# A two-layer convolution, attention and expert trunk: weight splits and sigmoids moved among the gate tiles

## The chip, the cores and the metric

The kernel runs on one core of one Trainium2 chip. The metric is the device time of the kernel in microseconds (us), from several timed executions; one more execution was recorded by the hardware profiler. The core has a matrix engine (TensorE, PE in the profile, its weight loads PEld), three engines for elementwise work (VectorE or DVE, ScalarE or ACT, GpSimd or POOL), SyncE (SP), whose queue issues most transfers here, and DMA engines that move data between HBM and the on-chip memory (SBUF). Matrix products land in PSUM banks. Each engine works through its own queue in order; semaphores order the engines among each other.

## The reference

The input is 256 tokens with 16 learned meta tokens ahead of them, 272 in all, with 1024 features. Two layers follow each other. Each has a mixer and an expert stage:

```
h = rmsnorm(x, mix_g);  z = h @ w_in            # conv_in, c_q, c_kv, k_rope, gate_logits
u = conv_in[:512] * sigmoid(conv_in[512:])
u = silu(layernorm(causal_depthwise_conv(u)))   # 31 taps
y_conv = u @ w_conv_out
o = chunk_causal_attention(q, k, v)             # 8 heads, low-rank q and kv, norms and rope
y_mla = o @ w_mla_out
gates = sigmoid(gate_logits)                    # 2048 columns: 16 tiles of 128
x = x + (gates[:1024] * y_conv + gates[1024:] * y_mla) @ w_out
x = x + peer(rmsnorm(x, ffn_g))                 # 16384 experts, the best 16 for each of 8 heads
```

All of it is float32. The result is the last 256 tokens after both layers.

## The kernel before

**Layout.** Activations lie transposed: features on the 128 partitions, tokens along the free axis, 272 of them in layer 0 and, from the gates on, 256 in layer 1 (the meta tokens are no longer needed there as outputs). A tile of a projection is 128 output features by all tokens, 8 matmuls over the 1024 input features (`ztile`, which takes one of three PSUM banks named `z`). Weights stream from HBM in pieces of 1 MB through a ring of four buffers (`wraw`), issued by SP in the order of use (`dma_to`, L86); a buffer is free again when both halves have been read.

**Order by hand.** The program is written with a manual schedule: the order of the instructions in the text is the order in each engine's queue. Work that runs beside the projections is written as Python generators, and each `next` puts the following step into the queues. `attention` and `layernorm` are such generators, and so is `conv2`, which does 21 of the 31 taps of one of the four channel groups as copies on ScalarE and accumulating transfers from POOL's queue.

**The gate loop** (L790) makes the 16 gate tiles of a layer. For each it does: the matmuls; on VectorE the product of the tile with the row's 1/rms (L792), which frees the PSUM bank; then, for i up to 11, two steps of attention with convolution taps between them; for i from 12 on, two steps of attention (which has nothing left by then) and two of layernorm. Attention's steps are the last ones of a loop over x from 0 to 10 (L570), two steps for each x: even x scores a pair of heads, mixes an earlier one, and applies the softmax (Exp on ScalarE); odd x transposes the probabilities (`turn`), copies them to SBUF (`put`) and scales the next pair. Gate i goes with x = i-1 here, so that x = 10 falls in i = 11, and x = 6 in i = 7.

**Sigmoids.** A tile's sigmoid (L787) runs in place on ScalarE. Exp and Sigmoid need different function tables, so the sigmoids wait for a flag, `vt["exp"]`, which attention sets when it is past its softmaxes. Before, it is set at x = 9 (L599). `gates(n)` does sigmoids in the order of the tiles up to number n; the loop asks for two more in each gate, and `gates(16)` does the rest behind the loop.

**Layernorm** (L697) normalizes the convolution's result over its 512 channels. Its steps: sums on PE; subtraction of the mean and squares; sums of the squares; 1/rms by three Newton iterations on VectorE (`rsqrt_steps`, L175 to L180, a step after each); products with it, and for each of four channel groups a Sigmoid and an Identity with scale and bias on ScalarE (L720 to L724); an empty step; the last products and the split of the result into a rounded part and its remainder (L728 to L731, `uk` in the profile). Before, the gates from i = 12 take two steps each.

**Projection tiles.** The output projections run as three products of rounded parts: high times high, low times high, high times low. For that a half piece of weights (128x1024) is split. `high(i, n)` rounds it on ScalarE (L666; n says how many uses ahead in the ring it lies) and `low(i)` computes the remainder on VectorE (L676). The parts go into buffers that other work has left: part 0 into `wuq`, part 1 into `seln` and `upad`, part 2 into `kh`, part 3 into `wuq` again, then on in turn with `acc` and `sqa` for i%3 = 2. `half_tile(i, src)` then makes two output tiles of 24 matmuls together, one in a `z` bank, one in an `aps` bank. I call this projection tile i. Tiles 0 to 3 are `w_mla_out` on attention's output (`sq` in the profile), tiles 4 to 7 `w_conv_out` on layernorm's (`uk`). After tiles 0 to 3 a product with the gate (L830) frees the banks; after tiles 4 to 7 `merge` (L843 to L848) multiplies by the other gate, adds, and splits the sum into `xh` and `kh` for the out projection (`three(8, ...)` and on).

Before, part 0 is made at i = 14, and parts 1 and 2 behind the gate loop, behind all sigmoids; part 3 is made in the projection loop behind tile 0.

After the mixer come the expert scores and the top-16 search, and then two long stages that stream the expert tables through PE while rows are gathered by POOL's queue.

Of the kernel before, what the change touches and what calls it, by code (L numbers as in the profile page):

```python
# [49 lines left out]
def trunk_kernel(ctx: ExitStack, tc: tile.TileContext, a: dict, out: bass.AP, dbg=None, stop=None):  # L50
# [39 lines left out]
    def peek_w(n):  # L90

        k = state["use"] + n
        return raws[k // 2][:, k % 2]
# [68 lines left out]
    def run_all(g):  # L162
        for _ in g:
            pass
# [32 lines left out]
    for l in range(NL):  # L197
        last = l == NL - 1
        t0 = META if last else 0
# [51 lines left out]
        for g in range(4):  # L251
            g_ = slice(32 * g, 32 * g + 2)
# [6 lines left out]
        else:  # L259

            p = zp.tile([128, 512], F32, name="z", bufs=3)
# [46 lines left out]
        vt = {}  # L308
# [12 lines left out]
        def attention():  # L321
# [95 lines left out]
            for i0, i1, n in ((0, 2, 128), (2, 3, 16)):  # L417
                d_ = xr[:n, 16 * i0:16 * i1].rearrange("p (i q a g) -> p i q g a", i=i1 - i0, q=2, a=2)
                k_ = xr[:n, 16 * i0:16 * i1].rearrange("p (i q g a) -> p i q g a", i=i1 - i0, q=2, g=4)
# [20 lines left out]
            for b in range(2):  # L440
                pbs = [aps() for _ in range(4)]
                for g in range(4):
                    g_ = slice(32 * g, 32 * g + 2)
# [11 lines left out]
            def score(p):  # L455
                b = [aps(), aps()]
                pss = [[b[e][:, 0:144] for e in range(2)], [b[e][:, 144:144 + T] for e in range(2)]]
                for e in range(2):
                    for i, (q0, n) in enumerate(QT[:2]):
                        mm(pss[i][e], qh[0:98, 2 * p + e, q0:q0 + n], kh[0:98, 2 * p + e, 0:q0 + n], True, True)  # L460
                return pss

            def softmax(p, pss):
                mx = mp.tile([128, 4], F32, name="mx", bufs=2)
                nb = mp.tile([128, 4], F32, name="nb", bufs=2)
                sm = mp.tile([128, 4], F32, name="sm", bufs=2)
                pr = [mp.tile([128, 2, 144], F32, name="pr0", bufs=2), mp.tile([128, 2, T], F32, name="pr1", bufs=2)]
                for e in range(2):
                    for i in range(2):
                        V.tensor_reduce(mx[:, 2 * i + e:2 * i + e + 1], pss[i][e], axis=AX.X, op=OP.max)  # L470
                V.scalar_tensor_tensor(nb.rearrange("p (i e) -> p i e", i=2), mx.rearrange("p (i e) -> p i e", i=2),
                                       -1.0, sc[:, 0:2, 2 * p:2 * p + 2], op0=OP.mult, op1=OP.mult)
                for e in range(2):
                    for i in range(2):
                        x = 2 * i + e
                        S.activation(pr[i][:, e], pss[i][e], AF.Exp, bias=nb[:, x:x + 1],
                                     scale=sc[:, i, 2 * p + e:2 * p + e + 1], accum_out=sm[:, x:x + 1])
                PR[p] = pr, sm
# [32 lines left out]
            def mix(p):  # L511
                t1, t2, t3 = TP.pop(p)
                po = aps()

                def o_(e):
                    return po[e * 64:e * 64 + 64, 16:272]

                def hs(e):
                    return slice((2 * p + e) * 64, (2 * p + e) * 64 + 64)

                for e in range(2):
                    mm(o_(e), vt[0][:, hs(e)], t1[:, e], True, False)
                for e in range(2):
                    mm(o_(e)[:, 128:256], vt[1][:, hs(e)], t2[:, e], False, False)
                for e in range(2):
                    mm(o_(e), vt[2][0:16, hs(e)], t3[:, e], False, True)
                return po

            def out_(p, po):
                S.activation(oo[:, 0, p, 16:], po[:, 16:272], AF.Copy)  # L530
                V.tensor_tensor(oo[:, 1, p, 16:], po[:, 16:272], oo[:, 0, p, 16:].bitcast(F32), op=OP.subtract)

            def meta_score():
                pm = aps()
                pmv = pm[0:16, 0:128].rearrange("p (h k) -> p h k", h=8)
                for h in range(NH):
                    mm(pmv[:, h], qh[0:98, h, 0:16], kh[0:98, h, 0:16], True, True)
                return pmv
# [31 lines left out]
            for x in range(11):  # L570
                p = x // 2
                if x % 2 == 0:
                    if p < 4:
                        ps = score(p)
                    if p >= 2:
                        po = mix(p - 2)
                    yield
                    if p >= 2:
                        out_(p - 2, po)
                    if p < 4:  # L580
                        softmax(p, ps)
                    yield
                else:
                    if 1 <= p < 5:
                        tr = turn(p - 1)
                    if not last:
                        if x == 1:
                            ms_ = meta_score()
                        if x == 5:
                            mt_ = meta_turn(ms_)  # L590
                        if x == 9:
                            meta_mix(mt_)
                    yield
                    if 1 <= p < 5:
                        put(p - 1, tr)
                    if p < 4:
                        scale(p)
                    else:
                        vt["exp"] = True  # L599
                    if not last and x == 1:  # L600
                        ms_ = meta_softmax(ms_)
                    yield
# [46 lines left out]
        def high(i, n):  # L649

            w_ = peek_w(n)
            x = {19: 3, 21: 4, 23: 1, 25: 2}.get(i, i % 3)
            if x == 0:
                t_ = mp.tile([128, 2, 1024], F32, name="wuq")
                hi, lo = t_[:, 0], t_[:, 1]
            elif x == 1:
                hi = mp.tile([128, 1024], F32, name="seln")
                lo = mp.tile([128, 1208], F32, name="upad")[:, 0:1024]
            elif i == 2 or x > 2:
                t_ = mp.tile([128, 8 * T], F32, name="kh" if x < 4 else "sq", tag="kh" if x < 4 else "sq")  # L660
                hi, lo = t_[:, 0:1024], t_[:, 1024:2048]
            else:
                hi = mp.tile([128, 4 * T], F32, name="acc")[:, 0:1024]
                lo = mp.tile([128, 4 * T], F32, name="sqa")[:, 0:1024]
            parts[i] = hi.bitcast(F32R), lo.bitcast(F32R), w_
            S.activation(parts[i][0], w_, AF.Copy)  # L666
            if i > 20:
                S.activation(parts[i][1], w_, AF.Copy, scale=-1.0)

        def low(i):  # L670

            hi, lo, w_ = parts[i]
            if i > 20:
                G.dma_start(lo, w_, accum_op=OP.add)
            else:
                V.tensor_tensor(lo, w_, hi.bitcast(F32), op=OP.subtract)  # L676
# [102 lines left out]

        gt = [big("g0", [8, T]), big("g1", [8, T])]  # L780
        ln = None
        ng = [0]

        def gates(n):
            while ng[0] < n:
                g_ = gt[ng[0] // 8][:, ng[0] % 8, t0:]
                S.activation(g_, g_, AF.Sigmoid)  # L787
                ng[0] += 1

        for i in range(16):  # L790
            z = ztile(t0)
            V.tensor_mul(gt[i // 8][:, i % 8, t0:], z, rs[:, t0:])  # L792
            if ln is None:
                next(att, None)
                taps(TAPS[i] // 2, 1)
                next(att, None)
                taps(TAPS[i] - TAPS[i] // 2, i % 2)
                if min(ck.values()) == KW and next(cvp, "end") == "end":
                    ln = layernorm()
            else:  # L800
                next(ln, None)
                next(att, None)
                next(ln, None)
                next(att, None)
            if "exp" in vt:
                gates(min(i + 1, ng[0] + 2))
            if i == 14:
                high(0, 1)
                low(0)
        gates(16)  # L810
        high(1, 1)
        run_all(att)
        conv(93)
        run_all(cvp)
        if ln is None:
            ln = layernorm()
        oo = vt["o"]
        low(1)
        high(2, 2)
        low(2)  # L820
        for i in range(4):
            ps = half_tile(i, oo)
            if i == 2:
                run_all(ln)
            if i < 3:
                high(i + 3, 2)
                low(i + 3)
            next(ln, None)
            for f in range(2):
                V.tensor_mul(gt[1][:, 2 * i + f, t0:], gt[1][:, 2 * i + f, t0:], ps[f])  # L830
            next(ln, None)
        run_all(ln)
        uu = vt["u"]

# [237 lines left out]
        for i in range(16):  # L1072
# [9 lines left out]
            if i % 3 == 1:  # L1082
                k = next(ahead, None)
# [464 lines left out]
```

## Time and profile before

| | |
|---|---|
| median of 3 runs | 1734.21 us (1732.22 to 1735.2) |
| the profiled execution | 1733.18 us, its span 1731.4 us |
| PE busy | 1694.2 us, 98% |
| DVE busy | 1148.1 us, 66% |
| ACT busy | 559.4 us, 32% |
| gate loop and projections of layer 0 | about 71 to 187 us from the span's start |
| the same of layer 1 | about 948 to 1057 us |

Times in the views are in us from the start of the span; a row of the order of time gives start, duration, engine, line, operation, what is written and read, and in brackets how long the engine was idle before it and what released it. The duration of one instruction contains some time that overlaps with the next on the same engine, so a chain of them is shorter than the sum. A line can be that of a helper: all matmuls have L58.

### The profile page before, as it was taken

How to read it: one execution, taken by the hardware profiler on the slowest of the kernel's cores; microseconds unless marked ns; L12 is line 12 of the kernel's file. 1: busy time of each engine (PE TensorE's matmuls, PEld its weight loads, DVE VectorE, ACT ScalarE, POOL GpSimd, SP SyncE). 2: the span in 40 equal slices, each digit the busy share in tenths (PEclk: the TensorE clock that was granted, in tenths of full speed). 3: DMA queues.
4: the chain of work that ended last, by engine and by line, in shares of the span. 5: the costliest groups of instructions: out<-in, count | busy, mean ns of one | idle time of the engine just before them, and what ended most of it. 6: DMA issues, size and time to landing. Idle time of an engine off the chain costs nothing.

```text
span 1731.4 us, 30489 instructions
## 1 busy us (share of the span) xinstructions
PE 1694.2 (98%) x11995; PEld 1603.0 (93%) x11995; DVE 1148.1 (66%) x2987; ACT 559.4 (32%) x1596; POOL 306.5 (18%) x352
## 2 busy tenths in 40 slices
PE   9998999999999999999999989999999999999998
PEld 7677999989999999999986879999999999999998
DVE  6686888887888544443456868897888885333332
ACT  3455633434554111000024546333355441000000
POOL 0000022222112222233200100212221113222120
PEclk9999999999999999999999999999999999999999
DMA  6353686999999999999962546969999999999995
GB/s 238 108 146 122 219 266 238 369 382 418 420 420 416 421 421 421 421 420 416 418 251 98 134 131 232 288 273 365 396 425 424 424 418 415 389 387 391 397 391 206
DMA packets 85231, 568.50 MB, mean 328 GB/s; under 512 B 9560, under 2 KB 14872, under 8 KB 17624
## 3 DMA queue, kind: packets, MB, share of 16 engines
q1 hardware_dynamic: 49488, 338.54, 49.5%
q0 software_dynamic: 34880, 227.41, 33.9%
q8 instruction: 94, 1.54, 0.4%
q10 hardware_dynamic: 720, 0.60, 0.1%
q14 instruction: 49, 0.40, 0.1%
HBM read 556.18 MB, written 1.05 MB: 322 GB/s over the span
## 4 chain that ended last, share of the span: by engine, by line
PE 75%; issue 9%; DMA 8%; DVE 4%; POOL 2%; ACT 2%; POOLq 0%; SPq 0%; ACTq 0%; DVEq 0%
PE po L58 27%; PE z L58 20%; PE A L58 20%; DMA wraw<-vn 6%; PE aps L58 4%; DMA gb<-uv,iww 2%; POOL gb L1314 2%; PE wp L58 1%; PE sc L58 1%; PE xp L58 0%; DVE gb L1339 0%; DVE va L1325 0%; DVE upad L676 0%; DVE rq_w L179 0%; DVE rq_w L178 0%
## 5 line engine op out<-in xcount | busy, mean ns | idle before, releaser
L58 PE MATMUL A<-xh,wraw 128*128 128x160 f32 x3776 | 534.8, 301 | 1.2 <-ACT idxT L944 1.2
L58 PEld LDWEIGHTS A<-xh,wraw 128*128 128x128 f32 x3776 | 517.7, 191 | 1.6 <-issue 1.6
L1339 DVE SCALAR_TENSOR_TENSOR gb<-gb,xr 128x1024 f32<-128x1024 f32 x208 | 254.5, 1223 | 397.1 <-DMA gb<-uv,iww 396.7
L1314 POOL DMA_INDIRECT gb<-uv,iww x208 | 223.7, 1076 | 526.5 <-DVE va L1325 377.0
L58 PE MATMUL po<-Xh,wraw 128*128 128x160 f32 x2080 | 286.9, 300 | 4.1 <-DMA wraw<-vn 3.4
L58 PEld LDWEIGHTS po<-Xh,wraw 128*128 128x128 f32 x2080 | 283.1, 190 | 6.7 <-DMA wraw<-vn 5.4
L58 PE MATMUL po<-X,wraw 128*128 128x160 f32 x2016 | 277.8, 300 | 4.7 <-DMA wraw<-vn 2.5
L58 PEld LDWEIGHTS po<-X,wraw 128*128 128x128 f32 x2016 | 274.3, 190 | 7.7 <-DMA wraw<-vn 5.1
L58 PE MATMUL z<-xg,wraw 128*128 128x272 f32 (+2 forms) x1152 | 268.7, 391 | 0.0
L1325 DVE SCALAR_TENSOR_TENSOR va<-gb,am,va 128x1024 f32<-128x1024 f32 x203 | 259.6, 1279 | 4.0 <-ACT am L1350 3.7
L58 PEld LDWEIGHTS z<-xg,wraw 128*128 128x128 f32 (+1 forms) x1152 | 211.5, 189 | 46.0 <-issue 7.6
L1349 ACT ACTIVATE am<-am 128x1 f32<-128x1 f32 x208 | 41.3, 199 | 591.3 <-DVE gb L1339 591.2
L1253 ACT ACTIVATE ohA<-ohE,wlo 128x128 f16<-128x128 f16 x320 | 105.2, 429 | 6.4 <-DVE ohE L1250 5.7
L1313 POOL COPY warm<-wraw 1x1 f32<-1x1 f32 x86 | 40.7, 473 | 320.8 <-DMA wraw<-vn 320.8
L626 DVE SCALAR_TENSOR_TENSOR acc<-upad,cols,acc 128x272 f32<-128x272 f32 (+1 forms) x198 | 84.2, 484 | 0.2
L1264 ACT ACTIVATE Xh<-wp 128x260 f32<-128x260 f32 (+18 forms) x80 | 25.0, 313 | 126.5 <-DVE Xh L1261 116.6
L1350 ACT ACTIVATE am<-am,iww 128x1 f32<-128x1 f32 x208 | 61.3, 295 | 6.8
L1250 DVE TENSOR_TENSOR ohE<-ioh,idxT 128x512 f16<-128x512 f16 x160 | 60.1, 416 | 0.0
L638 POOL DMA_DIRECT2D part<-cp x12 | 13.2, 1102 | 249.4 <-ACT cp L635 249.4
L58 PE MATMUL wp<-ohE,ohA 128*128 128x128 f16 x640 | 51.4, 219 | 2.5 <-DVE ohA L1251 2.5
L58 PEld LDWEIGHTS <-ohA 128*128 128x128 f16 x640 | 43.3, 97 | 7.8 <-DVE ohA L1251 3.2
L58 PE MATMUL A<-xh,we 128*128 128x160 f32 x320 | 45.3, 299 | 0.0
(401 smaller groups left out, 1750.2 us busy)
## 6 DMA issues: line engine op xcount, KB each, us to landing
wraw<-vn SPq DMA_DIRECT2D x128, 1024.0 KB, 10.6
wraw<-u SPq DMA_DIRECT2D x118, 1024.0 KB, 10.3
wraw<-w_in SPq DMA_DIRECT2D x27, 1024.0 KB, 6.2
wraw<-wq SPq DMA_DIRECT2D x16, 1024.0 KB, 5.0
we<-u SPq DMA_DIRECT2D x10, 1024.0 KB, 8.8
wraw<-w_out SPq DMA_DIRECT2D x8, 1024.0 KB, 5.3
wraw<-w_mla SPq DMA_DIRECT2D x4, 1024.0 KB, 4.7
wraw<-w_conv SPq DMA_DIRECT2D x4, 1024.0 KB, 4.8
```

Of the source, the lines that this page charges most:

```text
L58: PE.matmul(o, l, r, start=start, stop=stop, skip_group_check=True)
L626: V.scalar_tensor_tensor(acc[:, c, t0:], u_, weight(c, k), acc[:, c, t0:], op0=OP.mult, op1=OP.add)
L638: G.dma_start(part[:, :, t0:], u_[:, :, t0:], accum_op=OP.add)
L1250: V.tensor_tensor(E[q], ioh[:, None].to_broadcast(full), pairs(q, b), op=OP.is_equal)
L1253: S.activation(A_[1][:, t // 2, :, t % 2], E[0][:, t // 2, :, t % 2], AF.Copy, scale=wlo[:, 4 * b + t:4 * b + t + 1])
L1264: S.activation(x_, p[:, :, a:b].rearrange("p t j -> p j t"), AF.Copy, scale=1.0 / WS)
L1313: G.tensor_copy(warm[0:1], state["w"][0:1, 0:1])
L1314: G.indirect_dma_start(out=g_, out_offset=None, in_=a[f"uv{l}"], in_offset=bass.IndirectOffsetOnAxis(ap=iww[i].bitcast(I32)[:, m // 16, 0, ...
L1325: V.scalar_tensor_tensor(vac[i], r, m_, vac[i], op0=OP.mult, op1=OP.add)
L1339: V.scalar_tensor_tensor(u_, u_, 1.0, xrs[i], op0=OP.mult, op1=OP.mult, accum_out=m_)
L1349: S.activation(m_, m_, AF.Gelu_apprx_tanh)
L1350: S.activation(m_, m_, AF.Copy, scale=iww[i][:, m // 16, 1, m % 16:m % 16 + 1])
```

## The change

Four edits, the same for both layers:

- The flag for the sigmoids is set in attention at x = 6, behind the last softmax's Exp, instead of at x = 9.
- `gates(n)` keeps a list of the tiles that have no sigmoid yet, does n of them, and takes tiles 8 to 15 (the attention output's gates) ahead of tiles 0 to 7. It is called with 2 at the end of each gate, and with 3 in each step of the projection loop for what may be left.
- `high` and `low` of parts 0, 1 and 2 stand in the gate loop at i = 13, 14 and 15: `high` right behind the gate's product, `low` behind the steps of attention and layernorm, ahead of the sigmoids.
- Layernorm's steps in gates 12 to 15 are 2, 4, 0 and 1 instead of 2 each, so that the three Newton iterations follow each other without a gate between them. The empty step moves into the projection loop.

```
@@ attention, even x
                     if p < 4:
                         softmax(p, ps)
+                    if p == 3:
+                        vt["exp"] = True
@@ attention, odd x
                     if p < 4:
                         scale(p)
-                    else:
-                        vt["exp"] = True
@@ the gate loop
-        ng = [0]
+        todo = []
         def gates(n):
-            while ng[0] < n:
-                g_ = gt[ng[0] // 8][:, ng[0] % 8, t0:]
+            while n and todo:
+                n -= 1
+                k = max(todo, key=lambda k_: (k_ // 8, -k_))
+                todo.remove(k)
+                g_ = gt[k // 8][:, k % 8, t0:]
                 S.activation(g_, g_, AF.Sigmoid)
-                ng[0] += 1
+        lnk = 0
         for i in range(16):
             z = ztile(t0)
             V.tensor_mul(gt[i // 8][:, i % 8, t0:], z, rs[:, t0:])
+            todo.append(i)
+            if i > 12:
+                high(i - 13, 2)
             if ln is None:
...
             else:
-                next(ln, None)
                 next(att, None)
-                next(ln, None)
                 next(att, None)
+                for _ in range((2, 4, 0, 1)[lnk]):
+                    next(ln, None)
+                lnk += 1
+            if i > 12:
+                low(i - 13)
             if "exp" in vt:
-                gates(min(i + 1, ng[0] + 2))
-            if i == 14:
-                high(0, 1)
-                low(0)
-        gates(16)
-        high(1, 1)
+                gates(2)
         run_all(att)
...
         oo = vt["o"]
-        low(1)
-        high(2, 2)
-        low(2)
         for i in range(4):
             ps = half_tile(i, oo)
...
             next(ln, None)
+            gates(3)
```

## The prediction

> **What bounds the kernel now.** I read the page first, then TensorE's waits, then the granted clock in short stretches, and last the order of time around the gate tiles of each layer.
>
> ```profile
> span 1731.4 us, 30489 instructions
> ...
> PE 1694.2 (98%) x11995; PEld 1603.0 (93%) x11995; DVE 1148.1 (66%) x2987; ACT 559.4 (32%) x1596; POOL 306.5 (18%) x352
> ```
>
> TensorE works 98% of the span, so a gain must come from the 37 us it idles or from time in which it runs slow. Its waits (total us, times, longest):
>
> ```profile
> PE z L58 <- ACT seln L666: 10.4, 2, 5.2
> ...
> PE z L58 <- DVE upad L676: 1.8, 3, 0.7
> PE z L58 <- DVE wuq L676: 1.3, 2, 0.7
> ```
>
> These rows are what the change touches: in each layer projection tiles 0 and 1 wait for their split weights (`high` is L666, `low` L676), 13.5 us in all. The clock comes on top (columns: stretch, its us, busy us of PE, PEld, DVE, ACT, POOL, then clock, DMA share, GB/s):
>
> ```profile
> 154.60:157.80 3.20, 3.16 (x23) 2.94 (x23) 1.73 (x5) 2.37 (x5) 0.00 (x0) 1.00 0.85 302
> ...
> 166.00:168.20 2.20, 2.20 (x11) 2.20 (x11) 2.20 (x7) 1.34 (x4) 0.00 (x0) 0.50 0.94 391
> ```
>
> After the short wait (0.6 us, next view) the clock stays 1.00; after the 5.2 us wait that ends at 163.00 it is halved, to 168.2 at least, some 5 us. Layer 0 in order of time (start, us, idle before and its releaser in brackets):
>
> ```profile
> 146.60 0.44 DVE L713 TENSOR_SCALAR rq_x<-aps 128x272 f32<-128x272 f32 x1 [1.39 <-PE aps L58]
> ...
> 150.27 0.44 DVE L792 TENSOR_TENSOR g<-z,rq_ym 128x272 f32<-128x272 f32 x1 [1.12 <-PE z L58]
> ...
> 153.35 1.22 DVE L676 TENSOR_TENSOR wuq<-wraw,wuq 128x1024 fp32r<-128x1024 f32 x1
> ...
> 153.54 0.49 PE L58 MATMUL z<-sq,wuq 128*128 128x272 f32 x1
> ...
> 154.63 1.64 PE L58 MATMUL z<-sq,wuq 128*128 128x272 f32 x11 [0.60 <-DVE wuq L676]
> 154.84 1.49 DVE L720 TENSOR_TENSOR acc<-acc,rq_yl 128x272 f32<-128x272 f32 x4
> 155.37 0.62 ACT L723 ACTIVATE sqa<-acc,cols 128x272 f32<-128x272 f32 x1 [8.96 <-DVE acc L720]
> ...
> 160.00 2.01 ACT L787 ACTIVATE g<-g 128x272 f32<-128x272 f32 x6
> 161.91 1.04 ACT L666 ACTIVATE seln<-wraw 128x1024 fp32r<-128x1024 f32 x1
> ...
> 163.00 0.59 PE L58 MATMUL z<-sq,seln 128*128 128x272 f32 x1 [5.21 <-ACT seln L666]
> ...
> 166.39 1.49 DVE L728 TENSOR_TENSOR acc<-acc,sqa 128x272 f32<-128x272 f32 x4
> ...
> 167.80 1.49 DVE L731 TENSOR_TENSOR uk<-acc,uk 128x272 fp32r<-128x272 f32 x4
> ...
> 175.08 0.29 PE L58 MATMUL z<-uk,seln 128*128 128x272 f32 x1
> ...
> 176.37 1.23 DVE L676 TENSOR_TENSOR wuq<-wraw,wuq 128x1024 fp32r<-128x1024 f32 x1 [0.66 <-ACT wuq L666]
> ...
> 187.13 0.29 PE L58 MATMUL z<-xh,acc 128*128 128x272 f32 x1
> ...
> 190.65 1.02 DVE L848 TENSOR_TENSOR kh<-az,xh 128x272 fp32r<-128x272 f32 x2
> ```
>
> Part 1's copy (161.91) stands on ScalarE behind eight layernorm operations (155.37 to 160.00) and six sigmoids, and these behind 8.96 us in which ScalarE had nothing: layernorm waited for 1/rms. A projection tile takes (187.13-175.08)/4 = 3.01 us. Layer 1, the same places:
>
> ```profile
> 1018.61 0.42 DVE L713 TENSOR_SCALAR rq_x<-aps 128x256 f32<-128x256 f32 x1 [1.30 <-PE aps L58]
> ...
> 1025.13 0.47 PE L58 MATMUL z<-sq,wuq 128*128 128x256 f32 x1
> ...
> 1045.52 0.28 PE L58 MATMUL z<-uk,seln 128*128 128x256 f32 x1
> ...
> 1046.81 1.23 DVE L676 TENSOR_TENSOR wuq<-wraw,wuq 128x1024 fp32r<-128x1024 f32 x1 [0.68 <-ACT wuq L666]
> ...
> 1056.91 0.28 PE L58 MATMUL z<-xh,acc 128*128 128x256 f32 x1
> ...
> 1060.61 0.99 DVE L848 TENSOR_TENSOR kh<-az,xh 128x256 fp32r<-128x256 f32 x2
> ```
>
> **The change, part by part (layer 0).** Nothing is added or removed; the same instructions stand elsewhere in the queues.
>
> *Sigmoids and table.* The flag is now set behind the last Exp. By the order of the steps that falls in gate i=7 (the eighth, earlier than the title has it).
>
> ```profile
> 120.43 0.57 ACT L508 ACTIVATE t<-aps 16x512 f32<-16x512 f32 x1
> ...
> 123.15 1.45 PE L58 MATMUL aps<-t,vt 128*64 128x256 f32 x12
> ...
> 131.04 0.57 ACT L508 ACTIVATE t<-aps 16x512 f32<-16x512 f32 x1
> 131.63 1.28 ACT L787 ACT_TABLE_LOAD   x1
> 132.92 0.75 ACT L787 ACTIVATE g<-g 128x272 f32<-128x272 f32 x2
> ```
>
> The load (1.28) and two sigmoids (0.75) come ahead of `put(2)`, whose three copies then end at 120.43+0.57+2.03 = 123.03 instead of 121.00. The mixing matmuls that read them start at 123.15 and need the third copy only in their last third (near 124.1): no wait, about 1 us in hand. Without that cover it would cost up to 2 us. Two sigmoids per gate make 2x9 = 18 places for 16 by i=15, so none is left behind the gates (0.335 us each, from 2.01/6). On the load, the Trainium skill, "ScalarE: Activation LUTs", section "What ACT_TABLE_LOAD costs", adds a drain of about 1.38 us to 1.28. The rows above show none (131.04+0.57 = 131.61, load at 131.63). By the page the third copy would end near 124.4 and PE would wait some 0.3 us per layer; the sum goes by the rows.
>
> *1/rms in one piece.* In before its chain fills DVE from 146.60 to the start of `low(0)` at 153.35, with a gate product (0.36 to the next start) and 1.12 us of idle time inside; without these it ends at 151.9. `low(0)` follows and is ready at 153.1 (1.22; the next instruction starts after 1.14). PE wants tile 0 at 153.54: the 0.60 us wait goes, with 0.4 us in hand.
>
> *Parts 1 and 2 with the gates.* DVE goes on: gate 14 (0.36), `low(1)` (1.14), gate 15 (0.36), from 153.04 to 154.9; layernorm's four products (1.43), to 156.3; `low(2)`, to 157.5. The copies of `high(0)` to `high(2)` (0.95 each) lie in the 8.96 us of ScalarE idleness, so they cost nothing; outside that they would delay layernorm one to one. PE wants tile 1 at 156.55 (its `low` is ready at 154.6) and tile 2 at 159.56 (157.5): the 5.21 us wait goes, and with it the halved clock. Gates 14 and 15 leave PSUM 2 to 3 us later; their banks are wanted by tiles 1 and 2, not before 156.5. The parts' source weights:
>
> ```profile
> 134.02 0.33 SPq L86 DMA_DIRECT2D wraw<-w_mla  x1
> ...
> wraw<-w_mla SPq DMA_DIRECT2D x4, 1024.0 KB, 4.7
> ```
>
> the later of the two loads lands near 138.7, and `high(2)` reads it at 154. SP's queue keeps its order; loads that wait for these buffers only start earlier.
>
> *What is late next.* ScalarE starts layernorm's eight operations at 155.35 (first product), as before, and needs the same 4.63 us (155.37 to 160.00); sigmoid 15 (0.335) to 160.3; `high(3)` to 161.3. DVE has waited for it since 157.5 and does `low(3)` to 162.5. Only then comes tile 0's product with its gate, whose bank tile 3 wants: tile 3 starts at 162.9 instead of 162.57, a new wait of 0.3. DVE goes on: the gate pair to 163.2; layernorm's end, as long as before (166.39 to the end of the row at 167.80, 2.9), to 166.1; `low(4)` to 167.3; tile 1's gate product, whose bank tile 4 wants, to 167.65. Tile 4 starts at 167.8, a new wait of 1.9 behind tile 3's end (165.9), against 175.08: **7.3 us earlier**. But DVE must still do `low(5)` and five more gate products (1.14+5x0.36) before `low(6)`: 170.6 against 176.37. From `low(6)` to the end of the last merge DVE is full in before (176.37 to 191.67, 15.3 us), and the out projection needs that merge. 170.6+15.3 = 185.9 against 191.67: **5.8 us** are left. PE gets there at 167.8+12.05+4.5 (36 matmuls at 3.01/24) = 184.3 and waits 1.6.
>
> *Layer 1, the same steps* (2.85 a tile, (1056.91-1045.52)/4; the work on 256 columns in place of 272 at 0.96 of layer 0's): 1/rms from 1018.61, 5.1 us, to 1023.7, `low(0)` to 1024.9 against PE at 1025.13; products to 1028.0; layernorm on ScalarE 1027.2 to 1031.7; `high(3)` 1033.0; `low(3)` 1034.2; tile 3 at 1034.6, 0.9 later than wanted; layernorm's end 1037.6; tile 4 at 1039.3 against 1045.52 (6.2 earlier, new wait 1.9); `low(6)` at 1042.1 against 1046.81: **4.7 us**.
>
> *The unknown: the clock after waits of 1.6 to 1.9 us.* Below stands the 0.60 us wait with no loss, above:
>
> ```profile
> 374.43 0.44 PE L1232 MATMUL wp<-ident,ef 128*128 128x128 f32 x2 [2.47 <-DVE ef L1031]
> 375.78 0.33 PE L1232 MATMUL wp<-ident,ef 128*128 128x128 f32 x1 [0.91 <-DVE ef L1221]
> ...
> 377.00:378.00 1.00, 1.00 (x5) 1.00 (x5) 1.00 (x3) 0.00 (x0) 0.81 (x1) 0.50 0.56 229
> ```
>
> two waits of 3.4 us together, then half clock. The price lies between 0 and about 2 us per layer (5 us at half clock is 2.5 us lost; part of it hides in the 1.6 us that PE waits anyway). I take 0, since 1.9 is nearer to 0.6 than to 3.4. The Trainium skill, "TensorE: Matmul & The Clock Gate", section "Part 1: The HAM clock gate (the "warmup" mystery)", halves the clock after an idle window of some 3.4 us, free-running: by it too the sum has 0 here, but it warns of any new wait that grows to that size.
>
> *After the mixer.*
>
> ```profile
> 365.00:590.00 225.00, 217.60 (x1740) 213.08 (x1739) 183.53 (x373) 99.77 (x361) 45.51 (x45) 0.99 1.00 413
> ```
>
> In the expert stage PE (217.60 of 225) and DMA (share 1.00) are both full. Its start hangs on the mixer, and its transfers on buffers that the same work frees, so it starts earlier by what the mixer saves, and I take the gain as kept. If the transfers there didn't move with it, layer 0's 5.8 would be lost (that is case B).
>
> **Sum:** 5.8+4.7 = 10.5 us off the profiled execution's 1733.18 (1731.4 of span and 1.8 around it): 1722.7. The median of the runs is 1.03 above that execution: **1723.7 us**.
>
> **The rivals.**
> *A: DVE does not cut the gain.* If DVE keeps up in the merges, tile 4's 7.3+6.2 = 13.5 stays: 1720.7. With no new waits at all tile 4 would start four full tiles behind tile 0, at 165.6 and 1036.5, 18.5 us in all: 1715.7. For it: PE is the busiest engine. Against it: the last merge (190.65) ends where PE needs it already now.
> *B: part of it is lost.* Layernorm's end is no earlier than now (169.3 instead of 166.1), or the new waits halve the clock (2 us): 2 to 3 us per layer are lost from the 10.5 (or layer 0's 5.8, above): about 1728.7. For it: only 0.2 to 0.4 us in hand at `low(0)`, and a queue on DVE without gaps. Against it: every row of layernorm after the products starts within 0.3 us of before.
> *C: no gain.* The gate sigmoids are not what held part 1, or the flag does not work; 1734. Against it: nothing but those stood between 155.37 and 161.91.
> *D: slower.* ScalarE now alternates sigmoids with copies from gate 7 to 15. If each alternation reloaded the table, two loads (2.56) would stand ahead of attention's copies in each of gates 8 to 11, where 1 us is in hand: 1.6 us a gate on PE; and 2.5 us more ahead of layernorm's squares: 8.9 us per layer, 17.8 against the 10.5, so 1734.2+7.3 = 1741.5. It decides from 5.3 us per layer on. Against it: one load in before, at 131.63, and the six sigmoids at 160.00 stand between layernorm's operations and a copy without a second one.
>
> **How the numbers follow.** Forecast (8 to 13 us gained) 0.62; A (13 to 18) 0.15; B (3.5 to 8) 0.15; C 0.05; D 0.03. The clock's bound alone adds up to 4 us, and I trust each layer's chain to about 1 us: 1721.7 to 1727.7 for the forecast; to leave out no more than 2 in 10, the range reaches into A and B: 1718.5 to 1728.5. A measurement of this kernel tells about 0.2%, 3.5 us, from no change: faster 0.92 (forecast, A, B), same 0.05, slower 0.03.
>
> **What would show it.** One table load per layer, near 119; no wait of PE on L666's `seln`; PEclk at 1.00 from 153 to 190; tile 0 without a wait; new waits of PE before tiles 3 and 4 (0.3 and 1.9; 0.9 and 1.9) and 1.6 before the out projection's last two blocks; the last merge 5.8 and 4.7 us earlier. It is wrong if PE waits for attention's mixing (table load), if the clock falls to 0.50 behind tile 4, or if the mixer ends earlier and the span does not.

## The result and the profile after

The changed kernel takes 1721.61 us (median of four runs, 1720.96 to 1722.45) against 1734.7 us of the kernel before beside it (1732.22 to 1735.98): a ratio of 0.9927 with an interval of 0.9909 to 0.9944. The forecast was 1723.7 us. The profiled execution took 1721.62 us, 11.6 us less than the one before (1733.18).

First the page and TensorE's waits in the kernel after, to be read beside the first two fences of the prediction:

```profile
span 1719.8 us, 30493 instructions
...
PE 1689.0 (98%) x11995; PEld 1597.0 (93%) x11995; DVE 1147.7 (67%) x2987; ACT 559.6 (33%) x1596; POOL 304.9 (18%) x352
```

```profile
PE z L58 <- DVE g L831: 4.2, 4, 1.6
...
PE z L58 <- DVE wuq L676: 1.1, 2, 0.6
...
PE z L58 <- DVE upad L676: 0.7, 2, 0.4
```

The 10.4 us on `seln` are gone from the list. In their place stand four waits, 4.2 us in all, for the products with the gate (`g`, L831), which free a projection tile's bank. So 13.5 us of waits for split weights became 6.0 us, of which 1.8 are still for split weights. PE's busy time fell by 5.2 us (1694.2 to 1689.0) with the same 11995 matmuls: fewer of them ran at half clock. That figure changes from one execution to the next: in a second profiled execution of the kernel after it is 1691.8.

Layer 0 in order of time (start, us, idle before and its releaser in brackets):

```profile
118.39 0.52 ACT L635 ACTIVATE cp<-upad,cols 128x272 f32<-128x272 f32 x1
118.94 1.28 ACT L790 ACT_TABLE_LOAD   x1
120.23 0.75 ACT L790 ACTIVATE g<-g 128x272 f32<-128x272 f32 x2
...
122.04 0.57 ACT L508 ACTIVATE t<-aps 16x512 f32<-16x512 f32 x1
122.68 1.45 PE L58 MATMUL aps<-t,vt 128*64 128x256 f32 x12
...
146.13 0.44 DVE L713 TENSOR_SCALAR rq_x<-aps 128x272 f32<-128x272 f32 x1 [1.39 <-PE aps L58]
...
151.45 1.22 DVE L676 TENSOR_TENSOR wuq<-wraw,wuq 128x1024 fp32r<-128x1024 f32 x1
153.06 1.88 PE L58 MATMUL z<-sq,wuq 128*128 128x272 f32 x12
154.42 1.49 DVE L720 TENSOR_TENSOR acc<-acc,rq_yl 128x272 f32<-128x272 f32 x4
154.95 0.62 ACT L723 ACTIVATE sqa<-acc,cols 128x272 f32<-128x272 f32 x1 [0.51 <-DVE acc L720]
...
159.91 1.04 ACT L666 ACTIVATE wuq<-wraw 128x1024 fp32r<-128x1024 f32 x1
160.98 1.23 DVE L676 TENSOR_TENSOR wuq<-wraw,wuq 128x1024 fp32r<-128x1024 f32 x1 [3.94 <-ACT wuq L666]
162.70 1.75 PE L58 MATMUL z<-sq,wuq 128*128 128x272 f32 x12 [0.20 <-DVE g L831]
167.48 0.36 PE L58 MATMUL z<-uk,seln 128*128 128x272 f32 x1 [1.52 <-DVE g L831]
170.12 1.22 DVE L676 TENSOR_TENSOR wuq<-wraw,wuq 128x1024 fp32r<-128x1024 f32 x1
182.58 0.39 PE L58 MATMUL z<-xh,wuq 128*128 128x272 f32 x1 [0.42 <-DVE wuq L676]
184.09 1.02 DVE L850 TENSOR_TENSOR kh<-az,xh 128x272 fp32r<-128x272 f32 x2
186.91 0.39 PE L58 MATMUL z<-xh,upad 128*128 128x272 f32 x1 [0.30 <-DVE upad L676]
```

The mixing matmuls (122.68) and tile 0 (153.06) start without a wait. The next copy of weights that is late is part 3's (159.91, still behind layernorm's eight operations). VectorE waits 3.94 us for it and only then comes to the products that tiles 3 (162.70) and 4 (167.48) wait for. Layer 1:

```profile
1011.93 0.42 DVE L713 TENSOR_SCALAR rq_x<-aps 128x256 f32<-128x256 f32 x1 [1.30 <-PE aps L58]
...
1028.12 1.62 PE L58 MATMUL z<-sq,wuq 128*128 128x256 f32 x12 [0.81 <-DVE g L831]
1032.79 0.36 PE L58 MATMUL z<-uk,seln 128*128 128x256 f32 x1 [1.63 <-DVE g L831]
...
1048.95 0.99 DVE L850 TENSOR_TENSOR kh<-az,xh 128x256 fp32r<-128x256 f32 x2
```

**Where the 11.6 us lie.** Not all of it belongs to the change. The warm-up matmuls at the very start already differ between the two executions, here in the order of time of the kernel before and then of the kernel after:

```profile
2.01 5.06 PE L58 MATMUL z<-ones 128*128 128x128 f32 x22 [2.01 <-DVE strip L135]
```

```profile
2.01 4.30 PE L58 MATMUL z<-ones 128*128 128x128 f32 x22 [2.01 <-DVE strip L135]
```

Nothing of the change stands ahead of them. What is left of these 0.76 us when layernorm's `rq_x` is reached is 146.60-146.13 = 0.47. In the second profiled execution of the kernel after these matmuls took 5.06 us, and `rq_x` came at 146.69, so up to there the change gains nothing. To keep such offsets out, I measure the mixer from the start of its `rq_x` row to the start of its last merge's `kh` row. In layer 0 that is 190.65-146.60 = 44.05 before and 184.09-146.13 = 37.96 after, **6.09 less**; in layer 1 it is 42.00 and 37.02, **4.98 less**. Layer 1's `rq_x` comes 1018.61-1011.93 = 6.68 earlier, so layer 0's gain came through the expert stage whole (0.47+6.09 = 6.56), and 0.47+6.09+4.98 = 11.54 of 11.6 is accounted for.

The granted clock after the new waits (stretch, its us, busy us of PE, PEld, DVE, ACT, POOL, then clock, DMA share, GB/s):

```profile
156.20:165.90 9.70, 9.50 (x74) 9.14 (x73) 5.72 (x13) 7.23 (x15) 0.00 (x0) 1.00 0.66 258
167.40:170.50 3.10, 3.02 (x24) 3.05 (x25) 3.10 (x7) 0.36 (x1) 0.00 (x0) 1.00 0.18 24
```

It stays at 1.00, behind the 1.52 us wait too.

### The profile page after: what moved, and what is told of

It reads as the page before. It is cut to its first block, busy times and chain, and to the rows that moved or that the text cites. A ratio compares the mean times of both kernels' runs of the same rounds, so it can differ in the third digit from the quotient of the medians.

```text
span 1719.8 us, 30493 instructions
## 1 busy us (share of the span) xinstructions
PE 1689.0 (98%) x11995; PEld 1597.0 (93%) x11995; DVE 1147.7 (67%) x2987; ACT 559.6 (33%) x1596; POOL 304.9 (18%) x352
## 4 chain that ended last, share of the span: by engine, by line
PE 66%; DMA 13%; issue 8%; DVE 8%; ACT 2%; POOL 2%; SPq 0%; POOLq 0%; DVEq 0%; ACTq 0%
PE po L58 25%; PE z L58 17%; PE A L58 16%; DMA wraw<-vn 8%; DMA gb<-uv,iww 5%; PE aps L58 3%; POOL gb L1316 2%; PE wp L58 1%; DVE gb L1341 1%; DVE va L1327 1%; PE sc L58 1%; DVE wuq L676 1%; PE xp L58 0%; DVE upad L676 0%; DVE az L846 0%
## 6 DMA issues: line engine op xcount, KB each, us to landing
wraw<-u SPq DMA_DIRECT2D x118, 1024.0 KB, 10.2
```

## The experiments

Kernels 1 to 4 ran on one chip, 5, 6 and 8 with the kernel after on a second, 7 and 9 on a third, each group beside the kernel before. Across the groups I compare mixer lengths, each from one profiled execution; the two of the kernel after agree to 0.01 us. My theory was the prediction's: the places of parts 1 and 2, the early flag and the 1/rms in one piece each take away a delay that PE waits for, and the clock adds to the price of the long wait. The rivals were that one of the edits does nothing, or that the gain is mostly clock.

All of them in one table. The mixer lengths are taken from each kernel's own rows as above; the last two columns are what they are shorter than before's 44.05 and 42.00.

| kernel | median us | ratio to before, interval | mixer, layers 0 and 1 | shorter by |
|---|---|---|---|---|
| after (first result) | 1721.61 | 0.9927 (0.9909 to 0.9944) | 37.96, 37.02 | 6.09, 4.98 |
| after, again | 1722.01 | 0.9927 (0.9914 to 0.9941) | 37.95, 37.02 | 6.10, 4.98 |
| 1: 1/rms split | 1721.7 | 0.9934 (0.9917 to 0.995) | 37.93, 36.93 | 6.12, 5.07 |
| 2: flag late | 1726.31 | 0.9953 (0.9936 to 0.9969) | 39.79, 38.78 | 4.26, 3.22 |
| 3: parts late | 1732.1 | 0.9991 (0.9981 to 1.0001) | 43.47, 42.32 | 0.58, -0.32 |
| 4: before, clock held | 1731.08 | 0.9987 (0.9977 to 0.9996) | 42.29, 40.71 | 1.76, 1.29 |
| 5: part 3 early | 1715.54 | 0.9894 (0.988 to 0.9908) | 34.80, 33.60 | 9.25, 8.40 |
| 6: places of the parts alone | 1725.03 | 0.9944 (0.9929 to 0.9959) | 39.19, 38.12 | 4.86, 3.88 |
| 7: flag alone | 1731.18 | 0.9983 (0.9972 to 0.9993) | 42.85, 40.87 | 1.20, 1.13 |
| 8: part 7 early too | 1714.94 | 0.9886 (0.9871 to 0.9901) | 34.47, 33.58 | 9.58, 8.42 |
| 9: copies ahead of the mixing | 1732.23 | 0.9986 (0.9977 to 0.9996) | 37.93, 37.00 | 6.12, 5.00 |

Kernel 9's loss lies ahead of `rq_x` and so doesn't show in its mixer length.

**1: The 1/rms split again.** From the kernel after:

```
-                for _ in range((2, 4, 0, 1)[lnk]):
+                for _ in range((2, 2, 2, 1)[lnk]):
```

> The changed kernel with one edit undone: layernorm's steps in gates 12 to 15 are 2, 2, 2, 1, so that the Newton iterations are split by gate 14 again. Theory (VectorE's queue sets the mixer's pace from 1/rms on, and the amount of work in it is the same): low(0) now fills the idle time that the split had in the kernel before, layernorm's products start within 0.3 us of the changed kernel's 154.42 in layer 0, and the time is that of the changed kernel, 1721.6, within 1 us. Rival (the one piece is worth the gate product and the idle time, 1.5 us a layer): 1724.6.

It takes as long as the kernel after. In its order of time on VectorE:

```profile
146.62 0.44 DVE L713 TENSOR_SCALAR rq_x<-aps 128x272 f32<-128x272 f32 x1 [1.39 <-PE aps L58]
...
149.08 1.22 DVE L676 TENSOR_TENSOR wuq<-wraw,wuq 128x1024 fp32r<-128x1024 f32 x1
150.28 0.44 DVE L795 TENSOR_TENSOR g<-z,rq_ym 128x272 f32<-128x272 f32 x1
...
154.86 1.49 DVE L720 TENSOR_TENSOR acc<-acc,rq_yl 128x272 f32<-128x272 f32 x4
```

Here `low(0)` (149.08) fills the time in which before had idled 1.12 us ahead of the gate's product (150.27 there). Layernorm's products come 154.86-146.62 = 8.24 us after `rq_x`; in the kernel after it is 154.42-146.13 = 8.29, and before 154.84-146.60 = 8.24. So the piece is worth nothing. What takes tile 0's wait away is that `low(0)` stands one gate earlier.

**2 and 6: The flag late again, with 1/rms in one piece and split.** From the kernel after, and in 6 with the edit of 1 as well:

```
-                    if p == 3:
-                        vt["exp"] = True
 ...
                     if p < 4:
                         scale(p)
+                    else:
+                        vt["exp"] = True
```

> The changed kernel with the flag for the sigmoids set at x = 9 again; the order of the sigmoids and the places of the parts stay. Theory (the sigmoids matter only by what of them stands ahead of the parts' copies): four sigmoids of tiles 4 to 7 are left behind the gates, one more (0.34 us) stands ahead of high(3) and three (1.0 us) ahead of high(4), so tile 4 starts 1.3 us later in each layer: 1724.3. Rival (the backlog of sigmoids was what held part 1, and the flag is the main part of the gain): most of the 13 us is lost, 1730 or more.

> The changed kernel with only the places of the parts 0 to 2 changed (and the new order of the sigmoids): the flag at x = 9, layernorm's steps 2, 2, 2, 1. Theory (1/rms in one piece is worth nothing, the early flag some 4.7 us on top of the parts): as the kernel with the late flag, 1726.3 within 1 us. Rival (the three edits need each other): 1729 or more.

Kernel 6 is before with the new places of the parts and the new order of the sigmoids (those left over now stand behind the parts), and nothing else but the empty step's place: 4.86+3.88 = 8.74 us of the mixers' 11.07 come from that. The places were not timed without the new order; kernel 3 below has the order without the places and gains next to nothing. In both kernels tile 4 waits longer than in the kernel after, since two sigmoids in place of one stand on ScalarE ahead of part 3's copy, and more of them ahead of part 4's. TensorE's wait and the clock behind it, in kernel 2:

```profile
169.06 0.44 PE L58 MATMUL z<-uk,seln 128*128 128x272 f32 x1 [2.48 <-DVE g L831]
```

```profile
169.06:172.18 3.12, 3.12 (x14) 3.12 (x15) 3.12 (x7) 0.46 (x1) 0.00 (x0) 0.52 0.27 47
```

And in kernel 6:

```profile
169.88 0.37 PE L58 MATMUL z<-uk,seln 128*128 128x272 f32 x1 [2.48 <-DVE g L831]
```

```profile
169.88:173.00 3.12, 3.12 (x25) 3.12 (x26) 3.12 (x7) 0.46 (x1) 0.00 (x0) 1.00 0.33 42
```

The same wait of 2.48 us, and in the same 3.12 us behind it kernel 6 does 25 matmuls at a clock of 1.00, kernel 2 only 14 at 0.52. Layer 1 shows it again: waits of 2.55 in both, a clock of 1.00 in 6 and below it in 2. Up to there the two kernels keep step (tile 4 starts 169.06-146.44 = 22.62 and 169.88-147.29 = 22.59 us after `rq_x`), so the 0.60 and 0.66 us by which 2 has the longer mixers come behind that wait, with the clock. My expectation for 2 was 2.0 us too low (1724.3); this half clock, which it left out, is 1.26 of them by the profiled executions. For 6 I had expected 1726.3 within 1 us, and it came out 1.3 us lower.

**7: The flag alone.** Before with the flag of the change:

```
                     if p < 4:
                         softmax(p, ps)
+                    if p == 3:
+                        vt["exp"] = True
```

> The kernel before with the flag alone moved (x = 6 instead of x = 9); parts, order and layernorm as before. Theory (part 1's copy is held by layernorm, and of the six sigmoids ahead of it only five move away, 1.7 us): the copy starts 1.7 us earlier, PE waits 3.5 us instead of 5.2 ahead of tile 1, the clock still halves: 1731 to 1732.5. Rival (the six sigmoids held it): the wait is gone but for 1 us, 1724.

```profile
161.29 0.59 PE L58 MATMUL z<-sq,seln 128*128 128x272 f32 x1 [3.62 <-ACT seln L666]
```

With most of the sigmoids done earlier the wait of tile 1 shrinks from 5.21 to 3.62 us but stays, and with it the half clock. The mixers are 1.20+1.13 = 2.33 us shorter. With kernel 6's 8.74 that makes 11.07; both edits together, without the piece (kernel 1), give 6.12+5.07 = 11.19. In size the two edits add up, though the flag shortens another wait in each case: the one on `seln` when it is alone, those for `g` when the parts have moved.

**3: Parts 0 to 2 in their old places, the rest as after.**

```
-            if i > 12:
-                high(i - 13, 2)
 ...
-            if i > 12:
-                low(i - 13)
 ...
+            if i == 14:
+                high(0, 1)
+                low(0)
+        high(1, 1)
 ...
         oo = vt["o"]
+        low(1)
+        high(2, 2)
+        low(2)
```

> The changed kernel with the parts made where the kernel before made them: part 0 at gate 14, parts 1 and 2 behind the gate loop; sigmoids early and 1/rms in one piece. Theory (part 1's copy is held by layernorm's eight operations, not only by the sigmoids): the copy starts near 159.2 in layer 0, PE waits some 4 us ahead of tile 1 in each layer and the clock halves behind it; of the gain some 2.4 us a layer are kept: 1729.8. Rival (the sigmoids held it): the wait is under 1 us and the time within 3 us of the changed kernel's, 1722 to 1724.6.

In its order of time and its clock:

```profile
162.00 0.60 PE L58 MATMUL z<-sq,seln 128*128 128x272 f32 x1 [3.64 <-ACT seln L666]
```

```profile
166.00:168.00 2.00, 2.00 (x11) 2.00 (x11) 2.00 (x7) 1.44 (x4) 0.00 (x0) 0.50 1.05 434
```

The wait is 1.57 us shorter than before's 5.21, and next to nothing is gained (0.58 and -0.32; the interval of the ratio reaches 1). It is the flag, the new order and the piece without the places, and worse than the flag alone by 0.62 and 1.45 us. Tile 1 starts 162.00-146.72 = 15.28 us after `rq_x`, against 161.29-146.49 = 14.80 in kernel 7; in layer 1 it is 14.92 against 14.32. The clock is at 0.50 to about 168.4, 6.4 us behind the wait, against 6.2 in kernel 7; in layer 1 for 6.9 us, against 5.1. I expected 1729.8. So the shorter wait was paid back by a later tile 1 and by more work at half clock. If a us at half clock loses half a us, my estimate is 0.48+0.13 in layer 0 and 0.60+0.90 in layer 1, close to the 0.62 and 1.45.

**4: Before, with PE kept busy in the wait.** Twenty products of a tile of ones with itself, into a bank that nothing reads, behind tile 0:

```
             ps = half_tile(i, oo)
+            if i == 0:
+                wp_ = aps()
+                for _ in range(20):
+                    mm(wp_[:, 0:128], ones, ones, True, True)
```

> The kernel before with 20 dummy matmuls (128x128 by 128 columns, into a PSUM bank that nobody reads) behind projection tile 0, where PE waits 5.2 us for part 1. Theory (part of the cost of the wait is the clock that it halves): the dummies keep the clock at 1.00, tile 1 starts where it did, tiles 1 to 3 run at full pace and tile 4 starts some 2.4 us earlier in layer 0 and 1.8 in layer 1; at the mixer's end some 2 us a layer are left: 1730.5. Rival (the slow pace of tiles 1 to 3 is contention with the splits or with the transfers that start there, not the wait's clock): no change, 1734.5.

Its order of time and its clock:

```profile
162.91 0.39 PE L58 MATMUL z<-sq,seln 128*128 128x272 f32 x1 [0.75 <-ACT seln L666]
```

```profile
163.00:168.00 5.00, 4.13 (x31) 3.93 (x32) 5.00 (x8) 2.98 (x6) 0.00 (x0) 1.00 0.56 190
```

The weights come as late as before (162.91), but the clock stays at 1.00, and the mixers are 1.76+1.29 = 3.05 us shorter. So some 3 of the 11.07 us can be had by the clock alone, and the rival "mostly clock" falls; that the other 8 are the wait's own follows only if the two add up.

**5: Part 3 early too.** From the kernel after: part 3 in a buffer of its own (`xh`, which is free until the merges), its copy at i = 14 together with part 2's, and its remainder behind `low(2)` at i = 15:

```
+            if i == 3:
+                t_ = pp.tile([128, 8, T], F32, name="xh").rearrange("p a b -> p (a b)")
+                hi, lo = t_[:, 0:1024], t_[:, 1024:2048]
 ...
-            if i > 12:
+            if 12 < i < 15:
                 high(i - 13, 2)
+            if i == 14:
+                high(2, 3)
+                high(3, 4)
 ...
+            if i == 15:
+                low(3)
 ...
-            if i < 3:
+            if 0 < i < 3:
                 high(i + 3, 2)
```

> The changed kernel with part 3 made in the gate loop too, in the buffer xh, which nobody uses between attention's scores and the first merge: high(2) and high(3) at gate 14, in ScalarE's 6.6 us of idle time, low(3) at gate 15 behind low(2), where VectorE then waits 3.9 us for ScalarE. Theory (the new waits ahead of tiles 3 and 4 come from VectorE, which waits for high(3) behind layernorm, and VectorE's queue then sets the mixer's end): tiles 3 and 4 start without a wait, tile 4 2.4 us earlier in layer 0 and 2.9 in layer 1; the merges begin when tile 4 ends, so the last merge ends 3.0 and 3.7 us earlier: 1715. Rival (layernorm's end is what tile 4 waits for, and it does not move): both waits stay within 0.5 us, 1720 to 1721.6.

It beats both kernels, by 6.5 us against the kernel after on the same chip (1722.01 to 1715.54). On VectorE and, behind it, the windows of the same work, first of kernel 5, then of the kernel after:

```profile
157.18 1.23 DVE L679 TENSOR_TENSOR xh<-wraw,xh 128x1024 fp32r<-128x1024 f32 x1
...
181.15 1.03 DVE L858 TENSOR_TENSOR kh<-az,xh 128x272 fp32r<-128x272 f32 x2
```

```profile
152.90:184.00 31.10, 31.07 (x246) 30.73 (x244) 28.92 (x57) 17.70 (x30) 0.00 (x0) 1.00 0.57 203
```

```profile
152.90:187.00 34.10, 31.65 (x245) 30.75 (x243) 28.76 (x57) 20.24 (x32) 0.00 (x0) 1.00 0.52 185
```

PE is busy for 31.07 of 31.10 us: from tile 0 to the out projection there is no wait in layer 0. In the kernel after it idled 2.45 us of 34.10 (0.20+1.52+0.42+0.30 in the rows above). The two waits for `g` and both of the out projection's are gone, so part 3's copy behind layernorm was what held them all in layer 0. In layer 1 the two for `g` go as well, and the out projection's become shorter (0.63 and 0.43 to 0.33 and 0.44).

**8: Part 7 early as well.** From kernel 5: part 7 in `sq` (attention's output, read for the last time by tile 3), made behind tile 4 ahead of the merges.

```
-            x = {19: 3, 21: 4, 23: 1, 25: 2}.get(i, i % 3)
+            x = {7: 4, 19: 3, 21: 4, 23: 1, 25: 2}.get(i, i % 3)
 ...
-            high(i + 6, 1)
+            if i != 1:
+                high(i + 6, 1)
             if i:
                 merge(i - 1, prev)
-            low(i + 6)
+            if i != 1:
+                low(i + 6)
+            if i == 0:
+                high(7, 2)
+                low(7)
```

> The same with part 7 made ahead of the merges as well, in the buffer sq, which is free behind tile 3. Theory (from tile 4 on VectorE's 3.73 us per merge and split against 3.01 us per tile on PE set the end): one split of 1.14 us less between the merges makes the last merge end 1.1 us earlier in each layer: 1712.8. Rival (PE sets the end once part 3 is early): the same as with part 3 alone.

1714.94 against 1715.54, where 1712.8 was expected: no difference that the runs show, as the rival had it, and mixers shorter by 0.33 and 0.02 us. Where PE has no wait (layer 0), moving VectorE's work forward gives it nothing; in layer 1 the two waits of the out projection are 0.32 and 0.42 us, as in kernel 5 (0.33 and 0.44).

**9: What lies in hand at the sigmoids.** From the kernel after: eight copies on ScalarE behind the first two sigmoids in gate 7, into a gate tile that is not made yet.

```
+            if i == 7:
+                for _ in range(8):
+                    S.activation(gt[1][:, 7, t0:], rs[:, t0:], AF.Copy)
```

> The changed kernel with eight more copies (128x272, 0.335 us each, into a gate tile that is not made yet) on ScalarE behind the first sigmoids of gate 7, 2.7 us ahead of put(2). Theory (the table load and the first sigmoids are free because put(2) has about 1 us in hand): put(2)'s third copy ends at 125.3 instead of 122.6 in layer 0, the mixing matmuls behind gate 9 wait some 1.8 us in each layer, and the time is 3.6 us longer: 1725.4. Rival (there is more in hand than 2.7 us, and nothing waits): 1721.8.

Its order of time, layer 0 and layer 1:

```profile
121.26 3.64 ACT L818 ACTIVATE g<-rq_ym 128x272 f32<-128x272 f32 x8
...
125.85 2.60 PE L58 MATMUL aps<-t,vt 128*64 128x256 f32 x12 [2.72 <-ACT t L506]
...
1000.21 1.45 PE L58 MATMUL aps<-t,vt 128*64 128x256 f32 x12 [2.99 <-ACT t L506]
```

Its clock behind the one and the other wait:

```profile
125.80:128.40 2.60, 2.55 (x13) 1.09 (x13) 0.00 (x0) 2.60 (x8) 0.00 (x0) 0.50 0.60 246
...
1000.20:1001.60 1.40, 1.39 (x13) 0.68 (x13) 0.00 (x0) 1.40 (x5) 0.00 (x0) 1.00 0.83 345
```

The eight copies took 3.64 us, 0.455 each (I had counted with the sigmoids' 0.335), and PE waited 2.72: 3.64-2.72 = 0.92 us were in hand. In layer 0 the clock was then at 0.50 until 132.2, and `rq_x` comes 152.34-146.13-0.37 = 5.8 us later (0.37 is the offset at the start of this execution: its table load comes at 119.31). In layer 1 a longer wait, 2.99 us, left the clock at 1.00, and 3.7 us are lost (1021.83-1011.93, less 6.2 carried over). Together it is 9.5 us, and the median is 10.2 above that of the kernel after (1722.01, in another set of runs); 1725.4 was expected.

## Why the prediction was right

The sign and the range were right, and so was the mechanism: 5.8+4.7 = 10.5 us forecast, 6.09+4.98 = 11.07 measured in the mixers. Step by step in layer 0, with the measured times moved by the 0.47 us of the start:

| step | predicted | measured |
|---|---|---|
| table load and sigmoids in gate 7 | no wait, about 1 in hand | no wait; 0.92 in hand (kernel 9) |
| `low(0)` starts, tile 0 starts | 151.9, 153.54 | 151.92, 153.53 |
| layernorm starts on ScalarE | 155.35 | 155.42 |
| part 3's copy ends | 161.3 | 161.42 |
| tile 3: start, wait | 162.9, 0.3 | 163.17, 0.20 |
| tile 4: start, wait | 167.8, 1.9 | 167.95, 1.52 |
| `low(6)` starts | 170.6 | 170.59 |
| from `low(6)` to the last merge's end | 15.3 | 14.99 |
| waits at the out projection | 1.6, behind the merge | 0.42+0.30, for split weights |

In layer 1, with 6.68 us for what came ahead of it, tiles 3 and 4 wait 0.81 and 1.63 (0.9 and 1.9 predicted), the out projection 0.63 and 0.43, and the last merge is 4.98 earlier (4.7 predicted).

**Sigmoids and table.** There is one load per layer, at 118.94, so rival D (a reload at each alternation) is out; the groups of the kernel after by line give both layers together:

```profile
L790 ACT ACT_TABLE_LOAD x2 | 2.6, 1283 | 0.0
```

The Trainium skill's drain of about 1.38 us ("ScalarE: Activation LUTs", "What ACT_TABLE_LOAD costs") does not show here: the operation ahead of the load ends at 118.39+0.52 = 118.91, the load starts at 118.94, and the sigmoids start 1.29 us later. Rival C fell with kernel 7: the early flag shortens the wait, though alone it is worth only 2.33 us.

**1/rms in one piece.** The times of this step are right to 0.04 us, and its credit is wrong: "the 0.60 us wait goes" with the split 1/rms too (kernel 1). I counted the idle time that the piece closes and did not see that `low(0)`, moved forward, fills the same gap by itself. The step's 0.4 us in hand, which made rival B likelier, was no weakness either.

**Parts 1 and 2.** They are what the change lives on: 8.74 us without the flag and the piece (kernel 6). That copies in ScalarE's idle time cost nothing held: layernorm starts on ScalarE within 0.07 us of where it was put.

**What is late next.** Right in place and nearly in size. Part 3's copy behind layernorm makes the new waits, and VectorE's queue keeps 7.1 us at tile 4 from becoming more than 6.09 at the last merge. The term that was 0.3 us too high is VectorE's 15.3: before, it still held a wait of VectorE for ScalarE in the first merge, here in the order of time of the kernel before,

```profile
179.71 0.79 DVE L848 TENSOR_TENSOR kh<-az,xh 128x272 fp32r<-128x272 f32 x2 [0.46 <-ACT xh L845]
```

which the kernel after does not have. In layer 1 it is the same with 0.35 us. Without them the stretch is 0.31 us shorter in layer 0 and 0.20 in layer 1 (14.79 to 14.59), together most of the 0.57 us between 10.5 and 11.07. The 1.6 us before the out projection were put at the wrong work. PE waited there for `low(9)` and `low(10)`, which stand ahead of and behind the last merge in VectorE's queue, and not for the merge.

**The unknown clock.** Taking 0 for waits of 1.6 to 1.9 us was right, as they were 1.52 and 1.63 at a clock of 1.00. The reason given (a wait is nearer to 0.6 than to 3.4) suggests a length that decides, and there is none between 2.48 and 2.99: see the last section. By what is shown there, a wait of the 1.9 us predicted, whole in one step of the grid, leaves PE busy for 0.44 of it and could have gone either way, so part of this zero is luck.

**Rival A.** Its second case, "no new waits at all" at 1715.7, is kernel 5 at 1715.54. That the two agree so closely is in part luck: kernel 5's mixers are 17.65 us shorter, where 18.5 were counted. What I took for the limit of VectorE was the place of one more copy: with it moved, VectorE is out of the way and PE bounds the stage.

The 2.1 us between 1723.7 and 1721.61 are these 0.57, the 0.47 of the start, and the 1.03 by which I set the median above the profiled execution: the kernel after has its median at its profiled execution (1721.61 and 1721.62).

## What to carry to other kernels

Before an engine that idles behind a late operand is made faster, look in which queue the operand's preparation stands and what it could precede there: here the copies of two parts, 1 us each, stood behind eight layernorm operations, and their move into idle time, with part 0's remainder a gate earlier and the leftover sigmoids behind them, was worth 8.7 us. Then look for the next operand that is late for the same reason (part 3 gave 6.5 us more, with a free buffer as its only price), and stop when the waiting engine is busy throughout (part 7 gave nothing). Edits that come together should be timed apart: of the four here the places of the parts and the flag carry the gain, and the 1/rms in one piece carries none; the order of the sigmoids was never timed apart from the places.

## What was not expected of the hardware

**Which waits halve the clock.** In the mixers, waits of PE up to 1.63 us left it at 1.00, and all from 3.62 us on went with 0.50. Between them it went both ways: 2.48 and 2.55 in kernel 2 and 2.72 in kernel 9 halved it, 2.48 and 2.55 in kernel 6 and 2.99 in kernel 9 did not. So where a wait falls decides as well as its length.

The traces show more. Between the first and the last microseconds of a trace the half clock always lasts 3.41 or 6.83 us, whatever the wait, and may begin within it: in the kernel before from 161.42 to 168.25, in kernel 2 from 169.20 to 172.61. Within one execution its beginnings lie a whole number of steps of 3.413 us apart: 169.20, 370.58 and 1036.18 in kernel 2 are 59 and 195 steps. Put on this grid (kernel 6's clock falls at 370.36, 60 steps after 165.56), kernel 2's wait of 2.48 us lies whole in one step, and kernel 6's equal one is cut in two. First kernel 2, then kernel 6:

```profile
165.78:169.19 3.41, 0.93 (x8) 0.74 (x7) 2.41 (x6) 3.41 (x6) 0.00 (x0) 1.00 0.31 132
```

```profile
165.56:168.97 3.41, 1.84 (x15) 1.62 (x13) 2.41 (x6) 3.41 (x8) 0.00 (x0) 1.00 0.64 269
168.97:172.38 3.41, 2.50 (x20) 2.53 (x21) 3.41 (x8) 1.37 (x2) 0.00 (x0) 1.00 0.19 22
```

PE is busy for 0.27 of the step in kernel 2, and the next step runs at 0.50; in kernel 6 it is 0.54 and 0.73, and the clock stays. Over all steps at full clock in the twelve traces, each with a busy share below 0.41 was followed by half clock and none above 0.52 was; between these it went both ways (0.415 in kernel 9, layer 1, did not; 0.519 in kernel 5, at 371.51, did). In the kernel after the lowest share in the mixers is 0.53. The Trainium skill ("TensorE: Matmul & The Clock Gate", "Part 1: The HAM clock gate (the "warmup" mystery)") tells of a free-running window of some 3.4 us, and its free running fits that two equal waits end differently. That a whole idle window is needed does not fit kernel 2, where PE worked for 0.93 of the 3.41 us. What sets the grid's start in an execution, no run here shows.

**Copies are not as fast as sigmoids.** Eight copies of 128x272 in a row into one tile took 0.455 us each, while sigmoids of the same shape in place come 0.335 apart (six in 2.01 us). That the copies all write the same tile may be why; it wasn't tried.
